# Written order on three more engines, and the accumulating weight transfer one tile later, in an SSD and gMLP step

## The chip, the cores and the metric

The kernel runs on one core of a Trainium2 chip. The metric is the device time of one execution in microseconds. The kernel before takes 1185.45 us (median of 3 runs, 1184.87 to 1282.32).

## What is computed

One inference step through two layers over 640 tokens: 512 of a prompt, and 8 running streams of 16 tokens. The width is 1024. The first layer is a Mamba-2 SSD mixer, the second a gMLP with spatial gating.

```
proj = h @ w_in                                   # z | x | B | C | dt
xbc_c = silu(causal_dwconv(xbc, conv_prev, w, b)) # width 4
la = cumsum(dt * a); decay = exp(causal(la_t - la_s))
y_in = einsum('btsg,btsgr,bsgr,bsgrp->btgrp', C B^T, decay, dt, x)
y_st = C h * exp(la);  h_new = h * exp(last) + B (w dt x)
y = gated_group_rms_norm(y + d_skip * x, z); out = y @ w_out
# second layer: u, v, z = h @ w_in; v = layer_norm(gelu(v))
# out = (gelu(u) * (w_spatial v + b) * silu(z)) @ w_out
```

Each of the two layers adds its result to the trunk. The 32 heads lie in 8 groups that share B and C; the states before and after the step are inputs and outputs. All data is f32.

## The kernel before, in words

**Products.** An f32 product is made of three matmuls: both operands are split into a high and a low part (xH, xL; wh, wl), and high by high, low by high and high by low are added in PSUM. A projection of one weight tile (128 x 1024) over the 640 tokens is 48 such matmuls (pin), in two halves of the tokens.

**Weights.** The class Stream hands out weight tiles in a fixed sequence. `wsplit` (L94 to L100) fetches one: GpSimd issues a transfer of 512 KB to wh (L97); ScalarE writes wl = -wh (L98), rounded as wh is; GpSimd issues the same transfer again, this time adding to wl (L99). `next()` hands out a tile and issues what is missing up to three tiles ahead. There are four buffers each for wh and wl, so a tile's wh can only be issued when PE has read the tile four places before it. In the sequence of a full group stand x0, x1, B, C, z0, o, o, z1: the two o are tiles of the output projection of the group before. At the end of the sequence stand 16 tiles wBv of the gMLP's v projection; three of them are fetched this way, and never read as such, since gMLP makes its own splits: a transfer to raw, a copy to wh on ScalarE (L815), the rest to wl on VectorE (L816).

**A group of heads** runs over these steps. `conv_tile` (from L402) takes the projection of x0, x1, B or C: GpSimd clears and copies the edges of a buffer xp (L405, L406), VectorE scales PSUM into xp (L407 to L409), GpSimd copies the last tokens out as new cache (L411, L412), ScalarE and VectorE convolve to acc (L414, L417), and ScalarE's tanh and VectorE make xc (L423, L424). PE transposes xc to token order (tp, L464). `decay` makes four tiles E, each by a transfer, five instructions and an exponential on ScalarE (L510, L511). After the projection of z0 come five steps (the list `ssd`): `prompt_states(0)`, whose first instruction after PE's st is a copy to hs on ScalarE (L557); `old_states`, where VectorE fills cz (L571), PE makes yq, and GpSimd multiplies the old states h by their decay, eight times (L582); `cb_prompt`; `prompt_states(1)`; `cb_sample`. The output pieces (pop, ten of them, each followed by a sum into the trunk on VectorE, L681) lie between them. `mask` multiplies E by CBm, on VectorE, and one of the four on GpSimd (L626); `pair(0)` and `pair(1)` make yB and yA from them. Between the two pairs lie the last five output pieces. `gate` (th, y, yHL, L670 to L675) closes a pair; the projection z1 comes after `pair(1)`.

**What sets the order.** PE's order is the written one everywhere. In the SSD part a scheduler orders VectorE, ScalarE, GpSimd and SyncE; the gMLP part is in written order throughout. An engine takes its instructions, the transfers it issues among them, in its own order. In gMLP, `forms.next(n)` hands out a split weight and issues the splits up to n ahead (ScalarE L743, VectorE L744); `out_weights` (L962) calls it four times before the ten output pieces.

Of the kernel before, what the change touches and what calls it, by code (L numbers as in the profile page):

```python
# [15 lines left out]
P = 128  # L16
# [24 lines left out]
def hybrid_step(ctx: ExitStack, tc: tile.TileContext, xin, xT0, cst, wdt, cache, wA, wAo, h0in, wB, wBv, wBo,  # L41
# [49 lines left out]

    def wsplit(src):  # L94
        H = wpool.tile([P, 1024], F32R, name="wh", tag="wh", bufs=4)
        L = wpool.tile([P, 1024], F32R, name="wl", tag="wl", bufs=4)
        G.dma_start(out=H, in_=src)  # L97
        S.activation(L, H.bitcast(F32), AF.Identity, scale=-1.0)  # L98
        G.dma_start(out=L, in_=src, accum_op=ALU.add)  # L99
        return H, L  # L100

    class Stream:
        def __init__(self, srcs, ahead):
            self.srcs, self.ahead, self.got, self.n = srcs, ahead, [], 0

        def fill(self, ahead):
            while len(self.got) < min(len(self.srcs), self.n + ahead):
                i = len(self.got)
                self.got.append(wsplit(*self.srcs[i]))


        def first(self, n, between):
# [12 lines left out]

        def next(self, ahead=None):
            self.fill(1 + (self.ahead if ahead is None else ahead))
            r = self.got[self.n]
            self.got[self.n] = None
            self.n += 1  # L130
            return r
# [8 lines left out]
    def norm_first(zp, rb):  # L140
        xH, xL = norm_tiles()
        xt = zp.tile([P, KD, NT], F32, name="xt")
        nc.sync.dma_start(out=csb[0][:, :8], in_=cst[:, :8])
        nc.sync.dma_start(out=xt[:, 0, :], in_=xT0[0])
        dw = zp.tile([P, KD, HEADS], F32, name="dw")
        nc.sync.dma_start(out=dw, in_=wdt)
        dHL = zp.tile([P, KD, 2, HEADS], F32R, name="dHL")
        S.copy(out=dHL[:, :, 0], in_=dw)
        V.tensor_tensor(out=dHL[:, :, 1], in0=dw, in1=dHL[:, :, 0].bitcast(F32), op=ALU.subtract)
        W = stream.first(2, lambda i: [nc.sync.dma_start(out=xt[:, k, :], in_=xT0[k]) for k in ((1,), range(2, KD))[i]])  # L150
        nc.sync.dma_start(out=csb[0][:, 8:], in_=cst[:, 8:NCST1])
        acc = [zp.tile([P, NT], F32, name=f"sqa{i}") for i in range(2)]
        for k in range(KD):
            w = C("nw0")[:, k:k + 1]
            S.activation(xH[:, k, :], xt[:, k, :], AF.Identity, scale=w)
            V.scalar_tensor_tensor(xL[:, k, :], xt[:, k, :], w, xH[:, k, :].bitcast(F32), ALU.mult, ALU.subtract)
        stream.fill(1)
        warm = ps_op.tile([P, 512], F32, name="warm", tag="op")
        for _ in range(13):
            mm(warm[:, :P], ones, ones)  # L160
        pdt, px0 = [[pool.tile([P, 512], F32, name="pin", tag=tag)[:, :b - a] for a, b in HALVES]
                    for pool, tag in ((ps_y, "y"), (ps_in, "in"))]

        def dt_step(k):
            lw = dHL[:, k].rearrange("p a h -> p (a h)")
            for (a, b), o in zip(HALVES, pdt):
                mm(o[:64], lw, xH[:, k, a:b], start=(k == 0), stop=False)
                mm(o[:64], lw, xL[:, k, a:b], start=False, stop=(k == KD - 1))

        dt_step(0)  # L170
        for k in range(KD):
            if k + 1 < KD:
                dt_step(k + 1)
            for h in range(2):
                in_proj_step(W, (xH, xL), px0[h], h, k)
        dtT = zp.tile([64, NT], F32, name="dtT")
        for (a, b), o in zip(HALVES, pdt):
            S.copy(out=dtT[:, a:b], in_=o[:64])
        for k in range(KD):
            if k < 2:  # L180
                S.activation(acc[k], xt[:, k, :], AF.Square, scale=1.0 / 32)
            else:
                S.activation(xt[:, k, :], xt[:, k, :], AF.Square, scale=1.0 / 32)
                (V if k % 2 else G).tensor_tensor(out=acc[k % 2], in0=acc[k % 2], in1=xt[:, k, :], op=ALU.add)
        V.tensor_tensor(out=acc[0], in0=acc[0], in1=acc[1], op=ALU.add)
        rs = small.tile([P, TT], F32, name="rs0")

        def fin():
            pms = ps_m.tile([P, TT], F32, name="pms", tag="m")
            for t in range(TT):  # L190
                mm(pms[:, t:t + 1], acc[0][:, t * P:(t + 1) * P], ones[:, 0:1])
            V.tensor_copy(rs, rsqrt(pms, EPS, TT))
            ptd = ps_m.tile([P, TT, HEADS], F32, name="ptd", tag="m")
            for t in range(TT):
                mm(ptd[:, t, :], dtT[:, t * P:(t + 1) * P], C("sel")[:64])
            return ptd

        def half(a, b):
            pb = ps_m.tile([P, 512], F32, name="pb", tag="m")
            for t in range(a // P, b // P):  # L200
                dg = zp.tile([P, P], F32, name="dg", tag="dg", bufs=2)
                V.tensor_scalar(dg, ident, rs[:, t:t + 1], None, ALU.mult)
                mm(pb[:, t * P - a:(t + 1) * P - a], ones, dg)
            S.copy(out=rb[:, a:b], in_=pb[:, :b - a])

        return (xH, xL), px0, rs, fin, half
# [102 lines left out]
        names += [p[0] for p in part]  # L309
        units += [p[1:] for p in part]  # L310
    units += wo(GROUPS - 2) + wo(GROUPS - 1)
    units += [(wBv[i],) for i in range(16)]
    stream = Stream(units, 3)


    with ExitStack() as ca:
# [9 lines left out]
        ptds = []  # L326
        side.append(lambda: ptds.append(norm_fin()))
        side += [lambda h=h: norm_half(*h) for h in HALVES]
        px1 = in_proj(stream.next(), xT, ps_op, "op", at=(2, 10, 12))
        ptd = ptds[0]  # L330
        nc.sync.dma_start(out=csb[1], in_=cst[:, NCST1:])

# [69 lines left out]
        def conv_tile(o0, o1, ft, j, cch, nconv):  # L402
            xp = w1.tile([P, 667], F32, name="xp", tag="xp")
            xps = xp[:, 515:667].rearrange("p (b j) -> p b j", j=19)
            G.memset(xp[:, 0:3], 0.0)  # L405
            G.tensor_copy(out=xps[:, :, 0:3], in_=cch[:, j])  # L406
            V.tensor_tensor(out=xp[:, 3:387], in0=o0, in1=rb[:, 0:384], op=ALU.mult)  # L407
            V.tensor_tensor(out=xp[:, 387:515], in0=o1[:, 0:128], in1=rb[:, 384:512], op=ALU.mult)
            V.tensor_tensor(out=xps[:, :, 3:19], in0=o1[:, 128:256].rearrange("p (b j) -> p b j", j=16),  # L409
                            in1=rb[:, 512:640].rearrange("p (b j) -> p b j", j=16), op=ALU.mult)  # L410
            G.tensor_copy(out=nconv[:, j, 0, :], in_=xp[:, 512:515])  # L411
            G.tensor_copy(out=nconv[:, j, 1:9, :], in_=xps[:, :, 16:19])  # L412
            acc = w1.tile([P, 667], F32, name="acc", tag="acc")
            S.activation(acc[:, 0:664], xp[:, 0:664], AF.Identity, scale=cw[:, 4 * ft:4 * ft + 1],  # L414
                         bias=cw[:, 128 + ft:129 + ft])
            for k in range(1, 4):
                V.scalar_tensor_tensor(acc[:, 0:664], xp[:, k:k + 664], cw[:, 4 * ft + k:4 * ft + k + 1], acc[:, 0:664],  # L417
                                       ALU.mult, ALU.add)
            xc = w1.tile([P, NT], F32, name="xc", tag="xc", bufs=5)
            accs = acc[:, 515:667].rearrange("p (b j) -> p b j", j=19)[:, :, 0:16]  # L420
            xcs = xc[:, 512:].rearrange("p (b j) -> p b j", j=16)
            for o, a in ((xc[:, :512], acc[:, :512]), (xcs, accs)):
                S.activation(o, a, AF.Tanh)  # L423
                V.scalar_tensor_tensor(o, o, 1.0, a, ALU.add, ALU.mult)  # L424
            return xc

        cio = conv_io(0)
        pB = in_proj(stream.next(), xT, ps_y, "y")
        xcs = [conv_tile(*o, ft, j, *cio) for j, (o, ft) in enumerate(((px0, 0), (px1, 1), (pB, 16)))]
        side += [cum_sums] + [lambda h=h: by_heads(*h) for h in HALVES]  # L430
        pC = in_proj(stream.next(), xT, at=(2, 9, 11))
# [5 lines left out]

        xcs.append(conv_tile(*pC, 24, 3, *cio))
        pend = {}
        for g in range(GROUPS):  # L440
            last = g == GROUPS - 1
            hsl = slice(4 * g, 4 * g + 4)
# [340 lines left out]
    with ExitStack() as cb_:  # L783
# [162 lines left out]
        def then(n=1):  # L946
            for _ in range(min(n, len(later))):
                later.popleft()()
# [11 lines left out]
            V.scalar_tensor_tensor(h1[:, t, dsl], ps, 0.5, h1[:, t, dsl], ALU.mult, ALU.add)  # L960

        def out_weights():  # L962
            w = [forms.next(3) for _ in range(4)]
            return w[:2], w[2:]

        def out_piece(Ws, ys, p, after=None):
# [14 lines left out]
        for g in range(GROUPS):  # L981
# [9 lines left out]
            for i in range(2):  # L991
                f = 2 * g + i
                if i and 0 < g < GROUPS - 1:
                    Ws = out_weights()
                    for p in range(2 * TT):
                        out_piece(Ws, groups[g - 1], p)
                        then()
                uu = wk.tile([P, NT], F32, name="uu", tag="uu", bufs=2)
                zz = wk.tile([P, NT], F32, name="zz", tag="zz", bufs=1)
                pa, pb = (ps_m.tile([P, 512], F32, name="pqa", tag="m")[:, :HT],  # L1000
# [206 lines left out]
```

## Time and profile before

| | |
|---|---|
| profiled execution, its own time | 1181.53 us |
| span of its trace | 1179.4 us |
| busy PE / VectorE / ScalarE / GpSimd | 1053.0 / 826.2 / 447.1 / 228.2 us |
| granted clock of PE, mean | 0.96 of full speed |
| SSD part | 0 to 678 us |
| gMLP part | from 692 us on |

Busy time is the sum of an engine's instructions; a busy engine need not be at its peak. How the table is read: PE does most of the work, and the rows further on show where it waits, and for what. A row of a timeline gives the start, the duration, the engine, the line, the output and inputs, the count and, in brackets, the idle time before it with what ended it.

### The profile page before, as it was taken

The page shows a single profiled execution, that of the slowest core. Times are in us where ns is not written, and L with a number is a line of the kernel's source. Part 1 is how long each engine was busy: PE and PEld are TensorE (multiplying, and loading weights), DVE is VectorE, ACT ScalarE, POOL GpSimd, SP SyncE. Part 2 cuts the span into 40 slices and gives each one's busy share as a digit, 9 for nine tenths or more (in the row PEclk, how much of TensorE's full clock was granted, in tenths as well). Part 3 has the DMA queues.
Part 4 walks back from the last instruction along what each step waited for, and adds up shares of the span by engine and source line. Part 5 has one row for each costly group of instructions (what it writes and reads, how often), then busy time and mean ns, then how long its engine had stood idle before and what let it go on. Part 6 is the DMA issues. An engine that isn't in the chain of part 4 may idle for free.

```text
span 1179.4 us, 16944 instructions
## 1 busy us (share of the span) xinstructions
PE 1053.0 (89%) x6387; PEld 945.2 (80%) x6387; DVE 826.2 (70%) x1533; ACT 447.1 (38%) x804; POOL 228.2 (19%) x412
## 2 busy tenths in 40 slices
PE   7998998798889889987978949998899999999996
PEld 6987797697688678786977738887889889888985
DVE  4767866656747646756666766656788888788886
ACT  6354425244144153152252234334534333324343
POOL 3243413313314214224134100000000000000000
PEclk8898999999999989999998969998999999999998
DMA  9497676675575585676756642221124224223222
GB/s 321 108 247 196 142 200 155 137 231 135 121 232 126 132 230 136 144 200 145 207 143 155 213 115 72 72 81 50 52 81 129 67 70 125 82 82 97 84 63 89
DMA packets 66865, 161.08 MB, mean 137 GB/s; under 512 B 10176, under 2 KB 28864, under 8 KB 66784
## 3 DMA queue, kind: packets, MB, share of 16 engines
q0 software_dynamic: 19008, 69.21, 25.6%
q1 hardware_dynamic: 47776, 90.78, 24.6%
q8 instruction: 51, 0.84, 0.3%
q14 instruction: 30, 0.25, 0.1%
HBM read 143.11 MB, written 16.86 MB: 136 GB/s over the span
## 4 chain that ended last, share of the span: by engine, by line
PE 29%; DVE 22%; DMA 19%; issue 16%; ACT 8%; POOL 5%; SPq 0%; POOLq 0%; ACTq 0%; DVEq 0%
PE pv L69 9%; DMA wh<-wAo 7%; PE pop L69 6%; PE pin L69 5%; DMA wh<-wA 4%; DVE wf L744 4%; DMA dhl<-hl 3%; PE pqb L69 2%; DMA E<-laD 2%; ACT wl L98 2%; PE pqc L69 2%; DMA out_sspS<-h 2%; POOL wl L99 2%; DVE h L960 2%; PE pqa L69 1%
## 5 line engine op out<-in xcount | busy, mean ns | idle before, releaser
L69 PE MATMUL pin<-xH,wh 128*128 128x384 f32 (+1 forms) x768 | 252.5, 329 | 0.1
L69 PE MATMUL pin<-xL,wh 128*128 128x384 f32 (+1 forms) x768 | 241.8, 315 | 0.0
L69 PE MATMUL pin<-xH,wl 128*128 128x384 f32 (+1 forms) x768 | 241.7, 315 | 0.0
L69 PEld LDWEIGHTS pin<-xH,wh 128*128 128x128 f32 x768 | 149.8, 195 | 7.9 <-issue 4.3
L69 PEld LDWEIGHTS pin<-xL,wh 128*128 128x128 f32 x768 | 149.9, 195 | 0.2
L69 PEld LDWEIGHTS pin<-xH,wl 128*128 128x128 f32 x768 | 149.1, 194 | 0.0
L98 ACT ACTIVATE wl<-wh 128x1024 fp32r<-128x1024 f32 x66 | 69.9, 1059 | 192.0 <-DMA wh<-wA 102.2
L69 PE MATMUL pop<-wh,yHL 128*128 128x512 f32 x320 | 105.8, 412 | 22.8 <-DVE hs L561 13.1
L69 PE MATMUL pop<-wf,yHL 128*128 128x512 f32 x480 | 116.3, 398 | 8.7 <-DVE h L960 8.1
L417 DVE SCALAR_TENSOR_TENSOR acc<-xp,cw,acc 128x664 f32<-128x664 f32 x96 | 91.9, 957 | 35.1 <-ACT acc L414 33.5
L69 PEld LDWEIGHTS pop<-wf,yHL 128*128 128x128 f32 x480 | 88.8, 188 | 34.2 <-DVE h L960 12.8
L743 ACT CAST wf<-raw 128x512 fp32r<-128x512 f32 x128 | 76.7, 617 | 78.7 <-PE pop L69 28.8
L744 DVE TENSOR_TENSOR wf<-raw,wf 128x512 fp32r<-128x512 f32 x128 | 87.9, 692 | 25.0 <-ACT wf L743 22.6
L69 PEld LDWEIGHTS pop<-wh,yHL 128*128 128x128 f32 x320 | 58.6, 192 | 40.3 <-DVE hs L561 15.7
L424 DVE SCALAR_TENSOR_TENSOR xc<-xc,acc 128x512 f32<-128x512 f32 x64 | 35.5, 594 | 59.4 <-ACT xc L423 59.3
L99 POOL DMA_DIRECT2D wl<-wA x47 | 41.3, 878 | 176.6 <-ACT wl L98 151.5
L681 DVE SCALAR_TENSOR_TENSOR h<-pop,rr,h 128x512 f32<-128x512 f32 x80 | 59.3, 745 | 12.2 <-PE pop L69 12.1
L69 PE MATMUL pqa<-xH,wf 128*128 128x320 f32 x256 | 64.3, 320 | 3.2 <-ACT v L836 3.2
L69 PE MATMUL pqb<-tf,wf 128*128 128x320 f32 x384 | 64.1, 316 | 2.5 <-DVE zz L1022 2.5
L69 PE MATMUL pv<-wh,xL 128*128 128x512 f32 x160 | 63.4, 396 | 1.0 <-DVE xL L227 1.0
L69 PE MATMUL pop<-wl,yHL 128*128 128x512 f32 x160 | 64.0, 400 | 0.0
L69 PE MATMUL pv<-wh,xH 128*128 128x512 f32 x160 | 63.8, 398 | 0.0
(225 smaller groups left out, 2051.6 us busy)
## 6 DMA issues: line engine op xcount, KB each, us to landing
wh<-wA POOLq DMA_DIRECT2D x47, 512.0 KB, 6.6
wl<-wA POOLq DMA_DIRECT2D x47, 512.0 KB, 6.5
raw<-wB SPq DMA_DIRECT2D x32, 512.0 KB, 3.9
E<-laD SPq DMA_DIRECT2D x32, 320.0 KB, 6.5
h<-h0in SPq DMA_DIRECT2D x16, 512.0 KB, 5.2
out_sspS<-h SPq DMA_DIRECT2D x16, 512.0 KB, 6.6
wh<-wAo POOLq DMA_DIRECT2D x16, 512.0 KB, 5.8
wl<-wAo POOLq DMA_DIRECT2D x16, 512.0 KB, 5.6
```

The source lines that it names most:

```text
L69: T.matmul(out, lhsT=lhsT, rhs=rhs, start=start, stop=stop, **kw)
L98: S.activation(L, H.bitcast(F32), AF.Identity, scale=-1.0)
L99: G.dma_start(out=L, in_=src, accum_op=ALU.add)
L417: V.scalar_tensor_tensor(acc[:, 0:664], xp[:, k:k + 664], cw[:, 4 * ft + k:4 * ft + k + 1], acc[:, 0:664], ALU.mult, ALU.add)
L424: V.scalar_tensor_tensor(o, o, 1.0, a, ALU.add, ALU.mult)
L681: V.scalar_tensor_tensor(h1[:, t, dsl], ps, rg[:, t:t + 1], h1[:, t, dsl], ALU.mult, ALU.add)
L743: S.copy(out=t[:, 0], in_=src)
L744: V.tensor_tensor(out=t[:, 1], in0=src, in1=t[:, 0].bitcast(F32), op=ALU.subtract)
L960: V.scalar_tensor_tensor(h1[:, t, dsl], ps, 0.5, h1[:, t, dsl], ALU.mult, ALU.add)
```

## The change

GpSimd runs in written order through the whole program; VectorE and ScalarE do so from the loop over the groups on. SyncE stays with the scheduler. The transfer that adds to wl, and the copy ahead of it, are written in a new function `low`, called when the next tile's wh is about to be issued. Two early calls of `next` reach less far ahead. The 16 tiles wBv are gone from the sequence. In conv_tile the memset moves to VectorE, the three small copies move to ScalarE, two of them behind the acc instruction. In gMLP `out_weights` issues no splits ahead; they are issued after the pieces from the second on.

```diff
-    def wsplit(src):
-        H = wpool.tile([P, 1024], F32R, name="wh", tag="wh", bufs=4)
-        L = wpool.tile([P, 1024], F32R, name="wl", tag="wl", bufs=4)
-        G.dma_start(out=H, in_=src)
-        S.activation(L, H.bitcast(F32), AF.Identity, scale=-1.0)
-        G.dma_start(out=L, in_=src, accum_op=ALU.add)
-        return H, L
...
+        def low(self):
+            if self.half:
+                H, L, src = self.half
+                S.activation(L, H.bitcast(F32), AF.Identity, scale=-1.0)
+                G.dma_start(out=L, in_=src, accum_op=ALU.add)
+                self.half = None
 
         def fill(self, ahead):
             while len(self.got) < min(len(self.srcs), self.n + ahead):
-                i = len(self.got)
-                self.got.append(wsplit(*self.srcs[i]))
+                self.low()
+                src, = self.srcs[len(self.got)]
+                H = wpool.tile([P, 1024], F32R, name="wh", tag="wh", bufs=4)
+                L = wpool.tile([P, 1024], F32R, name="wl", tag="wl", bufs=4)
+                G.dma_start(out=H, in_=src)
+                self.half = H, L, src
+                self.got.append((H, L))
...
-    units += [(wBv[i],) for i in range(16)]
...
-        px1 = in_proj(stream.next(), xT, ps_op, "op", at=(2, 10, 12))
+        px1 = in_proj(stream.next(1), xT, ps_op, "op", at=(2, 10, 12))
...
-            G.memset(xp[:, 0:3], 0.0)
-            G.tensor_copy(out=xps[:, :, 0:3], in_=cch[:, j])
+            V.memset(xp[:, 0:3], 0.0)
+            S.copy(out=xps[:, :, 0:3], in_=cch[:, j])
...
-            G.tensor_copy(out=nconv[:, j, 0, :], in_=xp[:, 512:515])
-            G.tensor_copy(out=nconv[:, j, 1:9, :], in_=xps[:, :, 16:19])
             acc = w1.tile([P, 667], F32, name="acc", tag="acc")
...
+            S.copy(out=nconv[:, j, 0, :], in_=xp[:, 512:515])
+            S.copy(out=nconv[:, j, 1:9, :], in_=xps[:, :, 16:19])
...
-        pB = in_proj(stream.next(), xT, ps_y, "y")
+        pB = in_proj(stream.next(2), xT, ps_y, "y")
...
+        ca.enter_context(tc.manual_schedule(engines={mybir.EngineType.DVE, mybir.EngineType.Activation}))
         for g in range(GROUPS):
...
-            w = [forms.next(3) for _ in range(4)]
+            w = [forms.next(0) for _ in range(4)]
...
                         out_piece(Ws, groups[g - 1], p)
                         then()
+                        if p:
+                            forms.fill(min(p // 2 + 1, 4))
...
-    with _tile.TileContext(nc) as tc, tc.manual_schedule(engines={_mybir.EngineType.PE}):
+    with _tile.TileContext(nc) as tc, tc.manual_schedule(engines={_mybir.EngineType.PE, _mybir.EngineType.Pool}):
```

The first place is GpSimd in a full group, from the wl of a tile ahead of z0's end to the wh after `pair(1)`. Before, word for word (the first wh is that of the next x0, the pair of wh behind E those of the next x1 and B):

```order
L99 DMA wl<-wA 128x1024
L97 DMA wh<-wA 128x1024
L582 TENSOR_TENSOR h_1903<-h_1903,etot 128x256 x2
L582 TENSOR_TENSOR h_1905<-h_1905,etot 128x256
L582 TENSOR_TENSOR h_1903<-h_1903,etot 128x256 x2
L582 TENSOR_TENSOR h_1905<-h_1905,etot 128x256 x3
L99 DMA wl<-wA 128x1024
L626 TENSOR_TENSOR E<-E,CBm 128x640
L97 DMA wh<-wA 128x1024 x2
```

The same place in the change (the wh are those of z1, the next x0, the next x1, and, behind E, the next B):

```order
L112 DMA wh<-wA 128x1024
L103 DMA wl<-wA 128x1024
L112 DMA wh<-wA 128x1024
L103 DMA wl<-wA 128x1024
L112 DMA wh<-wA 128x1024
L591 TENSOR_TENSOR h_1903<-h_1903,etot 128x256 x4
L591 TENSOR_TENSOR h_1905<-h_1905,etot 128x256 x4
L635 TENSOR_TENSOR E<-E,CBm 128x640
L103 DMA wl<-wA 128x1024
L112 DMA wh<-wA 128x1024
```

The eight products and E moved from ahead of the wh of the next x1 to behind it, and the wh of the next B from beside that wh to behind the next wl.

The second place is ScalarE in a full group, from z0 to the first gate (th). Before, word for word:

```order
L98 ACTIVATE wl<-wh 128x1024
L423 ACTIVATE xc<-acc 128x512
L423 ACTIVATE xc<-acc 128x128
L466 COPY Bt<-tp 128x128
L486 CAST hl<-Bt 128x128
L557 COPY hs<-st 128x256
L98 ACTIVATE wl<-wh 128x1024
L670 ACTIVATE th<-zr 128x640
```

The same place in the change (the two wl are those of z1 and the next x0, the wl behind y that of the next x1):

```order
L475 COPY Bt<-tp 128x512
L475 COPY Bt<-tp 128x128
L495 CAST hl<-Bt 128x128
L497 CAST hl<-xw 128x256
L102 ACTIVATE wl<-wh 128x1024 x2
L566 COPY hs<-st 128x256
L679 ACTIVATE th<-zr 128x640
L301 ACTIVATE yHL<-y,csb_97 128x640
L684 ACTIVATE y<-y 128x640
L102 ACTIVATE wl<-wh 128x1024
```

The copy hs moved behind the wl of the next x0.

## Rows read from the trace of the kernel before

**Rows 1.** The tile yA in three stretches: count, duration in ns, first and last start.

```profile
L69 PE MATMUL yA<-E,xdt x16: 272/273/273, 158.8 to 159.6; 128*64 128x128 f32 x16
L69 PE MATMUL yA<-E,xdt x16: 272/272/273, 322.8 to 323.6; 128*64 128x128 f32 x16
L69 PE MATMUL yA<-E,xdt x16: 272/273/273, 571.2 to 572.0; 128*64 128x128 f32 x16
```

**Rows 2.** PE's waits from 323.9 to 377.7: total us, times, longest.

```profile
PE tp L464 <- DVE xc L424: 6.0, 2, 4.1
```

**Rows 3.** Timeline of PE, 376 to 409.

```profile
377.66 1.03 PE L69 MATMUL st<-xw,Bt 128*128 128x256 f32 x4
...
380.31 1.07 PE L69 MATMUL yq<-h,cz 128*32 128x256 f32 x16 [0.23 <-DVE cz L571]
...
389.32 0.73 PE L69 MATMUL pop<-wh,yHL 128*128 128x512 f32 x2 [2.98 <-DVE CBm L591]
...
393.31 0.73 PE L69 MATMUL pop<-wh,yHL 128*128 128x512 f32 x2 [2.34 <-DVE hs L561]
...
406.56 0.44 PE L69 MATMUL yB<-E,xdt 128*64 128x128 f32 x4
406.83 1.04 PE L69 MATMUL yA<-E,xdt 128*64 128x128 f32 x16
```

**Rows 4.** Timeline of ScalarE, 340 to 400.

```profile
350.88 1.06 ACT L98 ACTIVATE wl<-wh 128x1024 fp32r<-128x1024 f32 x1 [3.00 <-issue]
351.85 0.81 ACT L423 ACTIVATE xc<-acc 128x512 f32<-128x512 f32 x2
352.56 1.56 ACT L510 ACTIVATE E<-E,la 128x128 f32<-128x128 f32 x5
354.03 0.72 ACT L511 ACTIVATE E<-E 128x640 f32<-128x640 f32 x1
...
379.61 0.37 ACT L557 COPY hs<-st 128x256 f32<-128x256 f32 x1
388.30 1.06 ACT L98 ACTIVATE wl<-wh 128x1024 fp32r<-128x1024 f32 x1 [8.32 <-DMA wh<-wA]
```

**Rows 5.** Timeline of GpSimd, 325 to 412.

```profile
352.90 0.87 POOL L97 DMA_DIRECT2D wh<-wAo  x1
...
379.49 0.89 POOL L97 DMA_DIRECT2D wh<-wA  x1
381.02 4.90 POOL L582 TENSOR_TENSOR h<-h,etot 128x256 f32<-128x256 f32 x8 [0.64 <-PE yq L69]
...
390.55 1.69 POOL L626 TENSOR_TENSOR E<-E,CBm 128x640 f32<-128x640 f32 x1
405.20 1.26 POOL L97 DMA_DIRECT2D wh<-wA  x2 [12.97 <-PE pop L69]
```

**Rows 6.** PE's waits over the whole span: total us, times, longest.

```profile
PE pt L224 <- issue: 14.4, 1, 14.4
...
PE pop L69 <- DVE h L960: 8.1, 6, 1.3
...
PE pqc L69 <- DVE c L1016: 4.9, 5, 2.0
```

**Rows 7.** The page's transfers: count, KB each, median us from issue to landing.

```profile
wh<-wA POOLq DMA_DIRECT2D x47, 512.0 KB, 6.6
...
raw<-wB SPq DMA_DIRECT2D x32, 512.0 KB, 3.9
```

**Rows 8.** Timeline of GpSimd, 60 to 165.

```profile
133.86 0.87 POOL L99 DMA_DIRECT2D wl<-wA  x1 [5.24 <-ACT Bt L466]
134.41 0.43 POOL L405 MEMSET xp<- 128x3 f32 x1
```

**Rows 9.** Timeline of VectorE, 126 to 136, and 678 to 693.

```profile
129.37 2.80 DVE L417 SCALAR_TENSOR_TENSOR acc<-xp,cw,acc 128x664 f32<-128x664 f32 x3 [1.01 <-ACT acc L414]
...
682.82 1.22 DVE L816 TENSOR_TENSOR wl<-raw,wh 128x1024 fp32r<-128x1024 f32 x1 [7.88 <-DMA wl<-wBv]
```

More of the change, by code (lines that the diff above doesn't have):

```diff
@@ L90, in rsqrt @@
         return r
-    def wsplit(src):
-        H = wpool.tile([P, 1024], F32R, name="wh", tag="wh", bufs=4)
-        L = wpool.tile([P, 1024], F32R, name="wl", tag="wl", bufs=4)
-        G.dma_start(out=H, in_=src)
-        S.activation(L, H.bitcast(F32), AF.Identity, scale=-1.0)
-        G.dma_start(out=L, in_=src, accum_op=ALU.add)
-        return H, L
     class Stream:
         def __init__(self, srcs, ahead):
-            self.srcs, self.ahead, self.got, self.n = srcs, ahead, [], 0
+            self.srcs, self.ahead, self.got, self.n, self.half = srcs, ahead, [], 0, None
+        def low(self):
[4 more added lines that the diff above has]
+                self.half = None
         def fill(self, ahead):
             while len(self.got) < min(len(self.srcs), self.n + ahead):
-                i = len(self.got)
-                self.got.append(wsplit(*self.srcs[i]))
+                self.low()
[5 more added lines that the diff above has]
+                self.got.append((H, L))
         def first(self, n, between):
@@ L127, in next @@
             self.fill(1 + (self.ahead if ahead is None else ahead))
+            if len(self.got) == len(self.srcs):
+                self.low()
             r = self.got[self.n]
@@ L157, in norm_first @@
         stream.fill(1)
+        stream.low()
         warm = ps_op.tile([P, 512], F32, name="warm", tag="op")
```

## The prediction

> **What bounds the kernel now.** I read PE's waits first, then the timelines of PE, ScalarE and GpSimd over one group of heads, then the transfers. The SSD part is eight groups; a group ends with the second block of yA multiplications. Those of the second, fourth and seventh group end at 159.9, 323.9 and 572.3 us [rows 1] (the last start in each row plus 0.27). Five full groups lie between 159.9 and 572.3, so one takes 82.5 us. In the group from 323.9 PE's only wait before z0's last multiplication is for the activated convolution, xc: 6.0 us [rows 2]. ScalarE shows why: at 350.88 its copy wl had stood until its wh transfer was there, and the tanh of xc ran behind it, at 351.85 [rows 4]. After z0 come yq at 380.31 and waits of 2.98 and 2.34 for VectorE [rows 3]. One gap of 14.4 stands between SSD and gMLP, and gMLP has six short waits for h, 8.1 [rows 6]. In these stretches PE works without a break otherwise, so what PE waits for sets the time.
>
> **What the change removes.** The accumulating half of a tile now comes one tile later, just ahead of the next tile's wh. Its wh has then landed while PE ran a projection, so the xc waits should go: 6.0 in the group shown. The copies of conv_tile move to ScalarE: three per tile, each below the 0.37 of the larger hs copy [rows 4], so at most 1.1 a tile. Two of them stand behind the acc instruction, while VectorE needs 2.80 for its three acc steps [rows 9]; the third needs nothing of PE and is done early. I cost them at nothing; without this cover they would cost at most 32 times 1.1, 35 us. VectorE's memset goes the same way.
>
> **What written order adds.** Three places, all seen in the order of the change.
>
> *ScalarE before yq.* Two wl copies now stand ahead of the hs copy; before, hs was first. The second waits for the wh of the next x0, which GpSimd can only issue once z0 has been consumed by PE and after the preceding wl. VectorE's hs steps and h sum stand ahead of cz, which yq needs. From that issue to yq: landing 6.6 [rows 7], wl 1.06, hs copy 0.37, then four small VectorE steps, which I estimate from hs at 0.37 each: 9.5 us. Today hs ran at 379.61, and the wl that would stand ahead of it at 388.30 [rows 4].
>
> *GpSimd before the second pair.* The wh of x1 waits for the last out-projection piece that reads its buffer; it was issued at 405.20. Ahead of it, at 381.02 and 390.55, ran the eight h products (4.90) and the mask E (1.69) that the second pair needs [rows 5]. Now they stand behind it: 405.20 + 0.63 (half of the two issues) + 4.90 + 1.69 = 412.4, where PE's yB wanted E at 406.56 [rows 3]: a wait of 5.9. So from yq to the group's end I take 27.56 (380.31 to 406.83 + 1.04) less 2.98 and 2.34, which lie under the later yq, plus 5.9: 28.1.
>
> *The chain of transfers.* GpSimd alternates: wl of one tile (waits for ScalarE's copy, which waits for wh's landing), then wh of the next. One cycle is landing 6.6 [rows 7] plus copy and two issues: 350.88 (copy starts) to 352.90 (next wh issued) is 2.0 [rows 4, 5]. So c = 8.6. The four wh issues from 352.90 to 379.49 [rows 5] are 8.9 apart, so c is about this long already now. After the pair the next wl stands behind the first gate on ScalarE and VectorE: nine steps, about 0.7 each by the exponential of 128x640 [rows 4], 6.4, then copy and issues 2.0: the wh of B leaves 8.4 us after the group's end, where now two are issued together before it. From B six cycles (B, C, z0, two o, z1) lead to the wh of x0.
>
> So a group takes 8.4 + 6 x 8.6 + 9.5 + 28.1 = 97.6, against 82.5: **+15.1**, five times 75.5. Without the chain, z0 would end at 377.66 - 323.9 - 6.0 = 47.8; the chain reaches that point only at 60.0, so it decides.
>
> By the Trainium skill (DMA: Bandwidth & Descriptors, section Anatomy of one DMA — SWDGE (gpsimd) path) a transfer that GpSimd issues takes about 2.0 us plus its bytes at 436 GB/s, for 512 KB an estimate of 3.2; the trace has 6.6 for this very transfer. With 3.2 the chain would not decide (rival A).
>
> **Bounds of c.** Below: the 512 KB transfer raw<-wB lands in 3.9 [rows 7], c = 5.9. Above: the wh issued at 379.49 had its copy at 388.30, 8.8, c = 10.8. I take 8.6, since the median is over 47 transfers of the same kind.
>
> **The other parts.** *Second group* (the one that ends at 159.9): the two blocks alone give (9.5 - 2.65, the present way from z0's end to yq) + 5.9 = 12.8. Its four E decays now stand ahead of a wl: 4 x (1.56 + 0.72) = 9.1 [rows 4], plus a cycle: 30.5 at most. I take 22. *First group*: the decays stand there too; between 0 and 17.7 (9.1 + c); I take 10. *Last group*: it has no transfers to fetch behind hs and loses its xc waits; I take nothing, between -5.9 and +5.9 (one mask block). *Gap of 14.4*: VectorE stood 7.88 in it for the wl of a gMLP tile that is no longer fetched there [rows 9]; I take -8, between 0 and -14.4. *gMLP splits*: they stood between VectorE's h sums; spreading them over the pieces can remove the 8.1, or move it to the product pqc, which waits 4.9 now [rows 6]; I take -4, between -8.1 and +4.9.
>
> Sum: 75.5 + 22 + 10 + 0 - 8 - 4 = +95.5. The profiled execution took 1181.5 us, 0.3% below the median of the runs shown (1185.45). 1181.5 + 95.5 = **1277 us**.
>
> **Rivals.** *A, transfers land quickly.* If less traffic around them brings wh down to 3.9, the chain needs 8.4 + 6 x 5.9 = 43.8 and z0 decides at 47.8; yq comes at 47.8 + 9.5 - 2.7 = 54.6, the group ends at 82.7: +0.2. With the second group at 22 - 2 x 2.7 = 16.6 and the first at 7.3 the sum is 1 + 16.6 + 7.3 - 12 = +13: 1194. It holds below a landing of 4.6 ((47.8 - 8.4) / 6 - 2.0). For it: raw<-wB. Against it: wl and wh are issued back to back, and 47 of them show 6.6. By the skill's 3.2 a group would take 82.0, and the whole about 1191.
>
> *B, landings as long as the last one.* c = 10.8 makes a group 110.8: +141.5 for five, 1343. For it: 8.8 at 379.49. Against it: the median.
>
> *C, GpSimd's products pass a waiting transfer.* If a DMA that waits did not hold what stands behind it, the mask block would be gone and each wh would leave as its buffer comes free: group 47.8 + 9.5 + 22.2 = 79.5, -3.0; second group +6.9, first 0, the rest -12: 1181.5 - 15 + 6.9 - 12 = 1161. This decides from one point: whether an elementwise instruction starts while a DMA ahead of it waits. Against it: the memset of xp ran at 134.41, right behind the transfer issued at 133.86 after 5.24 us of waiting, though the VectorE acc steps that could hold its buffer had ended by 129.37 + 2.80 = 132.2 [rows 8, 9]. By the Trainium skill (TensorE: Matmul & The Clock Gate, section on the array's architectural detail) GpSimd's queue is strictly first in, first out; the memset agrees.
>
> **How the numbers follow.** Forecast (1240 to 1325, c from 7.4 to 8.9 with the other bounds): 0.62. Between A and it (1210 to 1240): 0.10. A: 0.13. B and worse: 0.08. C: 0.07. The range from 1190 to 1325 leaves out B and C, 0.15. Two per cent is about what a measurement of this kernel can tell from no change. Slower: 0.62 + 0.10 + 0.08 = 0.80; same: A, 0.13; faster: C, 0.07.
>
> **What would show it.** Right: tp's waits for xc nearly gone; PE's yq waiting 6 us or more for cz in every full group, with ScalarE's wl ahead of hs waiting for wh; yB waiting some 6 us for GpSimd's E, behind a wh that waited for pop; wh issues 8.6 apart after each pair; groups of about 98; the gap before pt at 6. Wrong: groups below 85, landings below 4.6, or E on GpSimd starting before the wh ahead of it was issued. The sum is most exposed to the landing: one us of it moves five groups by 35 us.

## The result

The changed kernel takes 1392.71 us (median of 4 runs, 1390.23 to 1395.19), before 1185.16 us; the ratio is 1.1769, with a 95% interval from 1.1722 to 1.1816. The median of the kernel before counts one execution of 1282.32 us in a slower state; the ratio leaves it out. The direction was forecast (slower), the size was not: 1277 was predicted, with 1325 as the upper end. The profiled execution's span is 1390.1 us against 1179.4, 210.7 more.

PE's waits over the whole span of the changed kernel (total us, times, longest):

```profile
PE yq L69 <- DVE cz L580: 103.5, 8, 16.8
PE yB L69 <- POOL E L635: 29.5, 6, 4.9
PE st L69 <- ACT Bt L475: 29.5, 6, 7.0
PE pin L69 <- DVE zr L548: 26.0, 2, 18.7
PE pin L69 <- DVE xp L414: 24.4, 8, 3.6
PE pin L69 <- DMA wl<-wA: 18.6, 11, 3.7
...
PE pt L232 <- issue: 1.6, 1, 1.6
```

No wait of tp for xc is left, and the gap ahead of pt [rows 6] is 1.6. Both were promised. In their place stand yq's waits for cz and yB's for GpSimd's E, at the very places that were forecast, and three kinds that were not: st for Bt, pin for zr and pin for xp.

The ends of the second, fourth, fifth, seventh and eighth group, read as with [rows 1] from the tile yA of the changed kernel (count, duration in ns, first and last start):

```profile
L69 PE MATMUL yA<-E,xdt x12: 420/421/421, 220.2 to 221.4; 128*64 128x128 f32 x12
L69 PE MATMUL yA<-E,xdt x12: 421/421/422, 446.7 to 448.0; 128*64 128x128 f32 x12
L69 PE MATMUL yA<-E,xdt x15: 420/421/421, 558.0 to 559.7; 128*64 128x128 f32 x15
L69 PE MATMUL yA<-E,xdt x12: 421/421/421, 781.4 to 782.7; 128*64 128x128 f32 x12
L69 PE MATMUL yA<-E,xdt x16: 272/272/273, 876.8 to 877.6; 128*64 128x128 f32 x16
```

Last start plus duration gives 221.8, 448.4, 560.1, 783.1 and 877.9; the first group ends at 125.8. The five full groups take 112.3 us each ((783.1 - 221.8) / 5) against 82.5. So the 210.7 us lie here:

| stretch | before | after | difference | predicted |
|---|---|---|---|---|
| up to the end of the first group | 106.3 | 125.8 | +19.4 | +10 |
| second group | 53.5 | 96.1 | +42.6 | +22 |
| five full groups | 412.4 | 561.2 | +148.8 | +75.5 |
| last group | 82.7 | 94.8 | +12.1 | 0 |
| from there to pt | 37.7 | 34.3 | -3.4 | -8 |
| from pt to the end | 486.8 | 477.9 | -8.9 | -4 |

One group, from 448.4 to 560.1, follows the predicted walk. GpSimd's timeline in it (the answers to [rows 5]):

```profile
455.99 0.88 POOL L112 DMA_DIRECT2D wh<-wA  x1
...
465.75 0.87 POOL L112 DMA_DIRECT2D wh<-wA  x1
...
495.94 0.88 POOL L112 DMA_DIRECT2D wh<-wAo  x1
...
507.21 0.89 POOL L103 DMA_DIRECT2D wl<-wAo  x1 [8.36 <-ACT wl L102]
...
516.76 0.90 POOL L103 DMA_DIRECT2D wl<-wA  x1 [8.09 <-ACT wl L102]
517.31 0.90 POOL L112 DMA_DIRECT2D wh<-wA  x1
...
551.03 0.55 POOL L112 DMA_DIRECT2D wh<-wA  x1 [22.00 <-PE pop L69]
551.59 4.60 POOL L591 TENSOR_TENSOR h<-h,etot 128x256 f32<-128x256 f32 x8
556.16 1.52 POOL L635 TENSOR_TENSOR E<-E,CBm 128x640 f32<-128x640 f32 x1
```

The wh of B leaves at 455.99, 7.6 us after the group's end (8.4 predicted). From there to the wh of the next x0 at 517.31 are six cycles, 61.3 us: 10.2 a cycle (8.6 predicted); the other four full groups, taken the same way, have 10.4 to 10.7. The last three rows are the block ahead of the second pair, as foreseen: 22.00 of waiting for pop, then the products and E. ScalarE and PE close the group, first ScalarE's timeline, then PE's:

```profile
505.75 1.04 ACT L102 ACTIVATE wl<-wh 128x1024 fp32r<-128x1024 f32 x1
...
515.28 1.06 ACT L102 ACTIVATE wl<-wh 128x1024 fp32r<-128x1024 f32 x1 [7.22 <-DMA wh<-wA]
526.67 1.06 ACT L102 ACTIVATE wl<-wh 128x1024 fp32r<-128x1024 f32 x1 [10.34 <-DMA wh<-wA]
527.63 0.35 ACT L566 COPY hs<-st 128x256 f32<-128x256 f32 x1
```

```profile
529.79 1.93 PE L69 MATMUL yq<-h,cz 128*32 128x256 f32 x16 [16.50 <-DVE cz L580]
...
557.73 0.47 PE L69 MATMUL yB<-E,xdt 128*64 128x128 f32 x1 [4.91 <-POOL E L635]
```

The hs copy stands behind a wl that waited 10.34 us for its wh, which landed some 9.3 us after its issue at 517.31. yq comes 12.5 us after that issue (9.5 predicted), the group's end 30.3 after yq (28.1 predicted). 7.6 + 61.3 + 12.5 + 30.3 = 111.7.

### The profile page after: what moved, and what is told of

The parts are those of the page before. It is cut to its first block, busy times and chain, and to the rows that moved or that the text cites. A ratio compares the mean times of both kernels' runs of the same rounds, so it can differ in the third digit from the quotient of the medians.

```text
span 1390.1 us, 16915 instructions
## 1 busy us (share of the span) xinstructions
PE 1093.6 (79%) x6387; PEld 973.8 (70%) x6387; DVE 828.7 (60%) x1565; ACT 456.4 (33%) x897; POOL 198.3 (14%) x278
## 3 DMA queue, kind: packets, MB, share of 16 engines
q0 software_dynamic: 18144, 66.07, 21.4%
## 4 chain that ended last, share of the span: by engine, by line
issue 35%; PE 30%; DVE 15%; POOL 10%; DMA 5%; ACT 4%; SPq 0%; POOLq 0%; DVEq 0%; ACTq 0%
PE pop L69 9%; PE pv L69 7%; DMA wh<-wA 4%; PE pin L69 3%; PE pqb L69 3%; POOL xw L485 3%; POOL h L591 2%; DVE wf L753 2%; POOL wl L103 2%; PE pqc L69 2%; POOL wh L112 2%; PE pqa L69 2%; DMA wh<-wAo 1%; DVE h L969 1%; ACT wf L752 1%
## 5 line engine op out<-in xcount | busy, mean ns | idle before, releaser
L69 PE MATMUL pin<-xH,wh 128*128 128x384 f32 (+1 forms) x768 | 258.4, 336 | 50.5 <-DVE zr L548 26.0
L69 PE MATMUL pin<-xH,wl 128*128 128x384 f32 (+1 forms) x768 | 246.9, 321 | 18.6 <-DMA wl<-wA 18.6
L69 PE MATMUL pin<-xL,wh 128*128 128x384 f32 (+1 forms) x768 | 245.6, 320 | 0.0
L69 PEld LDWEIGHTS pin<-xH,wh 128*128 128x128 f32 x768 | 152.7, 199 | 61.3 <-DVE zr L548 26.4
L424 DVE SCALAR_TENSOR_TENSOR acc<-xp,cw,acc 128x664 f32<-128x664 f32 x96 | 108.9, 1134 | 67.4 <-ACT acc L419 65.4
L102 ACT ACTIVATE wl<-wh 128x1024 fp32r<-128x1024 f32 x63 | 66.3, 1052 | 190.3 <-DMA wh<-wA 135.2
L69 PE MATMUL pop<-wh,yHL 128*128 128x512 f32 x320 | 111.9, 433 | 6.6 <-DVE h L690 6.6
L69 PE MATMUL yq<-h,cz 128*32 128x256 f32 x128 | 14.6, 603 | 103.5 <-DVE cz L580 103.5
L569 DVE TENSOR_TENSOR hs<-hs,etot 128x256 f32<-128x256 f32 x24 | 10.3, 430 | 119.5 <-ACT hs L566 119.2
L69 PEld LDWEIGHTS yq<-h,cz 128*32 128x32 f32 x128 | 4.6, 152 | 109.6 <-DVE cz L580 106.2
L69 PEld LDWEIGHTS pop<-wh,yHL 128*128 128x128 f32 x320 | 64.4, 208 | 21.9 <-DVE h L690 7.2
```

The lines of the kernel that those rows point to most:

```text
L69: T.matmul(out, lhsT=lhsT, rhs=rhs, start=start, stop=stop, **kw)
L569: V.tensor_tensor(out=hs[:, t], in0=hs[:, t - 1], in1=ev, op=ALU.mult)
```

## The experiments

My theory after the result: nothing but the written order costs time, and it does so where long work, or a transfer that waits, stands ahead of short work that PE waits for. The rivals: the transfer that adds, one tile later, is itself at fault; one engine's order alone is; or the chain alone is. The table has, for each run, the first group's end, the second group, a full group (mean of five) and the last, all from the yA tiles, and the time. Where a ratio is given below, it is to executions of the kernel before that ran alongside (medians 1180.2 to 1182.82); e2 to e6 and e11 are one execution each, and only differences far above the spread of the changed kernel's four (1390.23 to 1395.19) are read from them.

| run | first | second | full | last | time, us |
|---|---|---|---|---|---|
| before | 106.3 | 53.5 | 82.5 | 82.7 | 1185.16 |
| after | 125.8 | 96.1 | 112.3 | 94.8 | 1392.71 |
| e1, all but the written order | 105.8 | 59.6 | 82.3 | 79.1 | 1162.34 |
| e2, GpSimd written | 110.8 | 61.3 | 90.7 | 80.1 | 1218.78 |
| e3, VectorE and ScalarE written | 122.3 | 72.3 | 82.0 | 81.3 | 1195.02 |
| e4, wh ahead of wl | 119.1 | 83.5 | 97.1 | 85.8 | 1280.5 |
| e5, late fetches | 124.6 | 73.0 | 90.1 | 95.6 | 1258.2 |
| e6, e4 and e5 | 123.1 | 72.7 | 85.0 | 84.7 | 1213.35 |
| e7, e3 from the third group, decays late | 107.8 | 58.0 | 83.2 | 82.9 | 1168.68 |
| e9, e7 with late fetches and one earlier wl | 105.0 | 56.0 | 75.0 | 83.4 | 1127.95 |
| e10, e9 with GpSimd written, wh ahead of wl | 107.4 | 55.6 | 75.0 | 85.0 | 1129.57 |
| e11, after with decays late | 129.8 | 95.5 | 109.4 | 96.0 | 1381.94 |

**All edits but the written order.**

```diff
-        ca.enter_context(tc.manual_schedule(engines={mybir.EngineType.DVE, mybir.EngineType.Activation}))
...
-    with _tile.TileContext(nc) as tc, tc.manual_schedule(engines={_mybir.EngineType.PE, _mybir.EngineType.Pool}):
+    with _tile.TileContext(nc) as tc, tc.manual_schedule(engines={_mybir.EngineType.PE}):
```

> All edits of the change except the written order: GpSimd, VectorE and ScalarE stay with the scheduler. Theory 1 (the written order alone costs the time, by where it puts three things; the other edits are small gains): 1140 to 1175 us, faster than before by the gap between the parts (8 to 12), the gMLP waits (about 9) and some of the 27 us of xc waits. Rival (the transfer that adds, one tile later, is itself what makes weights late): above 1250 us.

1162.34 us, as expected, ratio 0.9845 (0.9789 to 0.9901): the written order costs 230 us, the other edits together gain about 18. The transfer that adds, one tile later, is not at fault. But it brings nothing in the full groups either, 82.3 against 82.5:

```profile
PE tp L470 <- DVE xc L430: 32.4, 10, 6.5
```

The waits for xc are about what they were (6.0 in the one group of [rows 2], 27.9 in the five full groups here, 5.6 each). The scheduler still puts a wl copy that waits for its transfer ahead of the tanh, as ScalarE's timeline shows:

```profile
276.14 1.06 ACT L101 ACTIVATE wl<-wh 128x1024 fp32r<-128x1024 f32 x1 [3.72 <-issue]
...
277.73 0.81 ACT L429 ACTIVATE xc<-acc 128x512 f32<-128x512 f32 x2
```

So the later transfer takes these waits away only together with ScalarE's written order: they stay in the next run, which leaves ScalarE to the scheduler, and are gone in the one after it, which does not.

**GpSimd alone in written order** (the change without the VectorE and ScalarE line of the diff above).

> The change with VectorE and ScalarE left to the scheduler; GpSimd in written order. Theory 1: the wait of yB for E on GpSimd (4.9 us, six times) stays, the chain of wl and wh on GpSimd stays, the wait of yq for cz (16 us in a full group) shrinks below 5, since the hs copy may pass the wl copies: 1290 to 1330 us. Rival (ScalarE's and VectorE's written order is all of it): below 1200 us.

1218.78, below the 1290 to 1330 expected. The block ahead of the second pair is there, in the amount of the changed kernel, 4.9 of the 8.2 us that a full group loses:

```profile
PE yB L69 <- POOL E L634: 29.5, 6, 4.9
PE tp L472 <- DVE xc L431: 27.2, 15, 6.9
...
PE yq L69 <- DVE cz L579: 3.4, 4, 1.8
```

yq hardly waits: with ScalarE scheduled, hs does not stand behind the wl copies, and GpSimd's chain of transfers does not set the group.

**VectorE and ScalarE alone in written order** (the change without the GpSimd part).

> The change with GpSimd left to the scheduler; VectorE and ScalarE in written order. Theory 1: yB's wait for GpSimd's E goes, yq's wait for cz stays at 8 to 16 us, since hs stands behind the two wl copies: 1270 to 1340 us. Rival (GpSimd's written order is all of it): below 1200 us.

1195.02, below the 1270 to 1340 expected, and below the 1200 that the rival named. But the rival's reason, that GpSimd's order is all of it, does not hold either: alone it costs 8 us a group. yq's waits are 6.2 in all, not 8 to 16 in a group. GpSimd's timeline shows why: the scheduler puts wh ahead of the wl of earlier tiles, each wh leaving as PE frees its buffer.

```profile
317.54 0.55 POOL L112 DMA_DIRECT2D wh<-wA  x1 [4.79 <-PE pin L69]
...
319.45 0.92 POOL L103 DMA_DIRECT2D wl<-wAo  x1
325.60 0.57 POOL L112 DMA_DIRECT2D wh<-wA  x1 [5.22 <-PE pin L69]
...
331.38 1.82 POOL L103 DMA_DIRECT2D wl<-wA  x2 [1.34 <-ACT wl L102]
```

So each order alone costs 8 us (GpSimd) or nothing (VectorE, ScalarE) in a full group, and both together 30. What the two make together, and neither alone, is, as I read it, the closed chain, which the next runs test: wl on GpSimd waits for ScalarE's copy, the next wh waits behind that wl, the next copy waits for that wh, and hs waits behind the copy. The loss of the first and second group, 19 and 43, is in good part VectorE's and ScalarE's: 16 and 19 here.

**The chain cut.**

```diff
             while len(self.got) < min(len(self.srcs), self.n + ahead):
-                self.low()
                 src, = self.srcs[len(self.got)]
...
                 G.dma_start(out=H, in_=src)
+                self.low()
                 self.half = H, L, src
```

> The change with one exchange in fill: the wh transfer of the next tile is issued ahead of the copy and the adding transfer of the tile before. So a wh no longer waits for ScalarE's copy. Theory 1: the chain of 10.2 us per tile is cut; a full group falls from 112 to about 91 us (z0's end at 48, yq 12.5 later, 30.3 from there), the whole to 1250 to 1290 us; waits of pin for wl<-wA vanish. Rival (the chain is not what sets the group, only the two blocks do): within 15 us of 1392.

1280.5, inside the range. But a full group falls from 112.3 to 97.1 and not to 91, and pin's waits for wl<-wA do not vanish (3.3 left of 18.6). yq's waits fall from 103.5 to 31.2. With the two blocks still there, the chain is worth 15 us a group, and this one exchange brings back 112 of the 207 us lost. The two transfers also change places in how long they take. After, then the exchange:

```profile
wh<-wA POOLq DMA_DIRECT2D x47, 512.0 KB, 7.4
wl<-wA POOLq DMA_DIRECT2D x47, 512.0 KB, 5.6
```

```profile
wh<-wA POOLq DMA_DIRECT2D x47, 512.0 KB, 5.4
wl<-wA POOLq DMA_DIRECT2D x47, 512.0 KB, 6.7
```

Each of these medians mixes transfers that leave alone with transfers that leave right behind another, so I sorted them by that. In the changed kernel 55 of the 63 wh leave within 0.9 us behind a wl, and all 55 land after it; the 39 of them from wA have a median of 7.7. In e4 nine wl from wA leave that close behind a wh, and all nine land after it, with a median of 7.2 for the wh's 4.2. What else is under way counts too. Three wh of the changed kernel, each with the stretch that was asked for: one alone (551 to 556), one behind a wl (495.9 to 502.5), and the one of 465.75, behind a wl while other transfers moved 1.41 MB (465.7 to 475.6):

```profile
wh<-wA POOLq DMA_DIRECT2D x1, 512.0 KB, 3.8
```

```profile
wh<-wAo POOLq DMA_DIRECT2D x1, 512.0 KB, 6.5
```

```profile
q1 hardware_dynamic: 552, 1.41, 46.6%
...
wh<-wA POOLq DMA_DIRECT2D x1, 512.0 KB, 9.7
```

(The q1 row has packets, MB and share of the queue for transfers that GpSimd does not issue.) In the full groups the five wh that leave alone land in 3.7 to 3.9. Of the 35 behind a wl, the 15 with at most 0.12 MB of other queues' traffic during their flight take 6.0 to 7.1, the 20 with 0.39 MB or more 7.3 to 11.1.

**The two blocks removed.**

```diff
-                Wo = [stream.next(), stream.next()]
+                Wo = [stream.next(2), stream.next(1)]
...
                 ssd[1]()
+                stream.fill(2)
                 ssd[2]()
...
             mask(1)
+            if 0 < g < GROUPS - 1:
+                stream.fill(3)
```

> The change with two fetches written later in the five full groups and the second: the wh of the next x0 (and wl of z1) behind old_states, the wh of the next x1 behind mask(1). So the hs copy has no new wl ahead of it, and the h products and E have no wh ahead of them that waits for an output piece. The chain wl to wh stays. Theory 1 (chain plus two blocks): yB's wait for GpSimd's E gone, yq's wait below 6; the chain then holds the o tiles, whose wl is needed for the piece ahead of yq: group 88 to 95 against 112, the whole 1240 to 1290. Rival (the chain alone sets the group): group above 105, above 1350.

1258.2, a full group 90.1, both as expected; yB no longer waits for GpSimd, and yq's waits are 12.2 in all. What is left over the whole span is st's waits for Bt (26.9), pin's for zr (24.3), for xp (23.7) and for wl<-wA (21.4). The next run, which also cuts the chain, shows which of them belong to it.

**Chain and blocks removed.**

> The late fetches and the exchange of wh and wl together, all still in written order. Theory 1: the 97 us per group that the exchange leaves, less the 5.3 of yq and the 5.8 of yB seen there: 84 to 88 a group, the whole 1195 to 1225 us. Rival (the time lies in ScalarE's own load, the E decays ahead of Bt): group above 93, above 1245.

1213.35, a full group 85.0, as expected. All three engines are still in written order, and 27 of the 30 us of a full group are gone. Against the run before, pin's waits fall from 23.7 to 7.2 for xp and from 21.4 to 10.6 for wl<-wA, so these were for the most part the chain's; st's for Bt and pin's for zr stay. With the blocks gone, cutting the chain is worth 5 us a group (90.1 to 85.0) where it was worth 15 with them: chain and blocks overlap, and their shares do not add up. What remains over the scheduled kernel is in the first two groups (123.1 and 72.7, against 105.8 and 59.6), in the last (84.7 against 79.1) and in st's waits for Bt, which stands behind two E decays on ScalarE:

```profile
PE st L69 <- ACT Bt L475: 31.5, 6, 5.6
```

**Written order from the third group on, GpSimd scheduled.**

```diff
+            if g == 2:
+                ca.enter_context(tc.manual_schedule(engines={mybir.EngineType.DVE, mybir.EngineType.Activation}))
...
-                queue(2, *((0, 1, 2, 3) if g == 1 else (2, 3)))
+                queue(2, *((0, 1, 2, 3) if g == 1 else (2, 3) if last else ()))
...
                 ssd[1]()
+                if g > 1:
+                    decay(2)
+                    decay(3)
                 ssd[2]()
```

> GpSimd left to the scheduler; VectorE and ScalarE in written order from the third group on, not from the first; and the decays of E for the third and fourth head written behind old_states instead of ahead of the Bt copies. Theory 1 (written order costs only where long work stands ahead of short work that PE waits for): the first two groups as scheduled, st's wait for Bt (4 us a group) gone, full groups 77 to 81: 1130 to 1155 us. Rival (the wait moves to E or to the output weights): full groups 82 or more, 1160 or more.

1168.68, ratio 0.9905 (0.9874 to 0.9937). The first two groups are back (107.8 and 58.0), and st's waits for Bt are gone. But the full groups stay at 83.2 and the time is above the range: a miss. The rival's numbers came, though not quite its reason: the wait moved to the output weights only in part, and most of it to yq, six times:

```profile
PE yq L69 <- DVE cz L581: 28.9, 6, 5.9
PE pop L69 <- DMA wl<-wAo: 12.4, 6, 2.9
```

ScalarE had Bt out early, and then stood with hs behind the second wl again.

**That wait removed too.** The late fetches are added, and the wl copy of the second o tile moves ahead of C's convolution:

```diff
                 o = in_proj(stream.next(), xT, at=(3, 7, 11, 14))
+                if g > 1:
+                    stream.low()
                 xcs.append(conv_tile(*o, 24 + g, 3, *cio))
```

> As the run with VectorE and ScalarE written from the third group on and the two decays behind old_states, now with the fetches of the next x0 and x1 written late (behind old_states, behind mask) and the wl copy of the second o tile ahead of C's convolution. GpSimd stays scheduled. Theory 1: yq's wait for cz (5.5 in a full group, hs behind two wl copies) and pop's wait for wl of the o tile (2.4) go: full groups 74 to 77, the whole 1125 to 1145 us. Rival (PE's other work or the landing of wl takes their place): full groups 80 or more, 1155 or more.

1127.95, ratio 0.9565 (0.9524 to 0.9606): faster than both kernels. A full group takes 75.0, 7.5 us less than before the change. In the group from 236.4 to 310.7 PE waits 4.2 us in all:

```profile
PE pin L69 <- DMA wl<-wA: 1.4, 2, 1.2
PE yB L69 <- DVE E L642: 1.0, 2, 0.7
PE yq L69 <- DVE cz L583: 0.9, 1, 0.9
PE pop L69 <- DMA dhl<-hl: 0.9, 1, 0.9
```

**The same with GpSimd written as well,** from the third group on, and wh ahead of wl:

> The same with GpSimd in written order too, from the third group on, and the wh of a tile issued ahead of the wl before it. Theory 1: with nothing long ahead of what PE waits for, written order on GpSimd costs nothing either: within 10 us of the same kernel with GpSimd scheduled, 1125 to 1150. Rival (written order on GpSimd costs 9 us a group whatever stands where): 1170 or more.

1129.57, ratio 0.9564 (0.9521 to 0.9608), a full group 75.0. In the full groups of this kernel written order on three engines costs nothing, once what waits stands behind what is awaited. The run makes two edits at once, so it does not show what each would do alone.

**How much of the cycle is ScalarE's lateness.** The changed kernel, with only the two decays moved behind old_states (as in the diff of the run from the third group on):

> The change with one move: in the full groups the E decays of the third and fourth head stand on ScalarE behind old_states instead of ahead of the wl copy of the second o tile. Theory 1 (the chain takes 10.2 us per tile, because a wh that is issued behind a wl lands in 7.4, and because in two of six cycles ScalarE is late by 1.4 and 3.3): the 3.3 goes and st's wait for Bt, 4 us, goes under: full groups 107 to 109 against 112, the whole 1365 to 1380 us. Rival (ScalarE's lateness does not matter, since the landing ends later anyway): within 5 us of 1392.

1381.94 and 109.4 a group: 2.9 of the 3.3 us expected in a group, the time 2 us above the range. The waits of st for Bt fell from 29.5 to 11.8 in all, while yq's stayed at 102.2 (103.5 before the move) and pop's for the wl of the o tiles rose from 8.3 to 16.5. So the earlier st brought nothing of its own: PE waits at the next places of the chain instead.

**Two parts alone, on the kernel before.** Without the wBv tiles (the line `units += [(wBv[i],) for i in range(16)]` deleted):

> The kernel before without the 16 gMLP tiles at the end of the fetch sequence, nothing else. Theory 1: the gap before pt falls from 14.4 to some 3, with VectorE's wait of 7.9 for wl<-wBv gone, the rest as before: 8 to 13 us faster, 1167 to 1175. Rival (the gap has another cause, the h sums of the last output pieces): within 3 us of before.

1169.92, ratio 0.9906 (0.9873 to 0.994), as expected; the gap ahead of pt, 14.4 before [rows 6], is 1.6.

With only the gMLP splits moved between the pieces:

> The kernel before with the gMLP splits between the output pieces, nothing else. Theory 1: the six waits of pop for h, 1.35 each, go and no other wait grows: 6 to 10 us faster than before, 1173 to 1178. Rival (the waits move to the product pqc or pqb): within 3 us of before.

1170.67, ratio 0.9916 (0.9892 to 0.994). That is 10.0 less than the 1180.67 alongside, at the upper end of the 6 to 10 expected; the time itself lies below the range, which was reckoned from a slower median of the kernel before. Of the six waits for h (8.1) 0.2 is left, and pqc's are 4.3 against 4.9 [rows 6].

## Why the prediction was right or wrong

**Right: the mechanism and its places.** hs behind the wl of the next x0, E behind the wh that waits for pop, and the chain of wl and wh between them were read from the order, and the trace has all three; e4, e5 and e6 take them away and give back 27 of the 30 us of a full group. Rival C fell: the products started at 551.59, right behind the wh that had waited 22.00 us for pop, though yq had freed the old states at about 531.7. So did rival A: the landing went up, not down. The xc waits went, as the first part said. One term at nothing held only because other waits covered it: the copies and the memset of conv_tile. pin waits 24.4 for xp in the changed kernel; in the full groups that lies ahead of yq's wait and, by e6, belongs mostly to the chain.

**Wrong: the length of the cycle, and with it the range.** Of the 210.7 us, 95.5 were predicted. The other 115 are 73 in the five full groups, 30 in the first two, 12 in the last, and 5 in the gap, less 5 that the gMLP splits gave beyond their term. Of the 29.8 us that a full group lost, 15.1 were predicted. In the group shown the terms are: cycle 10.2 for 8.6 (six times 1.6, 9.7), issue to yq 12.5 for 9.5 (3.0), yq to the end 30.3 for 28.1 (2.2), the gate 7.6 for 8.4 (-0.8): 14.1 in all. The step that failed is "landing 6.6 ... So c = 8.6", with the copy taken as never late. By cause, the landings are 7.2 of the 14.1: 7.4 on average in the six cycles (4.5 in all) and 9.3 ahead of yq (2.7), both for 6.6. A late ScalarE is 4.7, PE's clock 2.2, and the rest cancels.

- *The median was of the wrong mixture.* 6.6 was the median of 47 wh transfers issued in any company before. The prediction says that wl and wh are issued back to back and that 47 of them show 6.6; but only 14 of the 47 left right behind a wl, and these had a median of 7.9, the other 33 one of 5.1. In the changed order every wh of the cycles leaves 0.6 us behind a wl. So the longer landing could have been read before the change, and the traffic of the other queues belongs to it (e4). No run takes that traffic away, so its share is not measured by itself.
- *Rival B came close by luck.* Its group of 110.8 is near the measured 112.3, but it rests on a cycle of 10.8, where 10.2 was measured; and its step to yq kept the landing of 6.6, though 8.8 was its own premise (with it: 113.0). B also had no late ScalarE and no slower clock. It was given 0.08, together with what is worse.
- *ScalarE is part of the cycle.* I took the copy to be waiting for the landing. In two of six cycles ScalarE itself is late, behind the exponentials: the wl copies at 493.87 and 505.75, which let the transfers of 495.34 and 507.21 go, start 1.4 and 3.3 us after their wh had landed. The second share was taken away by a run, which gave back 2.9 us a group (e11).
- *The clock of PE.* I costed nothing for it. From yq to the end of the group PE is busy 24.50 us for 22.27 in the same 141 instructions, and the granted clock is 0.84 of full speed for 0.94. From yq to the group's end, in the two groups shown, the rows are, before and after:

```profile
380.30:407.90 27.60, 22.27 (x141) 17.89 (x141) 18.63 (x31) 3.18 (x4) 8.57 (x13) 0.94 0.58 125
```

```profile
529.80:560.20 30.40, 24.50 (x141) 19.47 (x141) 14.71 (x27) 0.74 (x1) 6.64 (x10) 0.84 0.18 46
```

(Columns: the stretch, its us, busy us and instructions of PE, PE's weight loads, VectorE, ScalarE and GpSimd, granted clock, share and GB/s of the transfers.) The 2.2 us by which the step from yq missed are just this: PE's idle time in it is 5.90, where the estimate was 5.9, all of it for yB, whose wait is 4.91.

**Wrong: the first, second and last group.** I had bounded the first two by four decays and a cycle, and the last by one mask block. The first shows what was overlooked, VectorE's own order: the copy hl stood 15.22 us for ScalarE, which had the decays and a wl first, and zr stood behind it, while PE waited 18.66 for zr to empty its PSUM.

```profile
79.87 0.29 DVE L496 TENSOR_TENSOR hl<-Bt,hl 128x128 fp32r<-128x128 f32 x1 [15.22 <-ACT hl L495]
...
84.31 0.88 DVE L548 TENSOR_TENSOR zr<-pin,rb 128x384 f32<-128x384 f32 x2
```

I had followed the queues of ScalarE and GpSimd, and of VectorE only the steps ahead of cz. e7 and e3 set against each other show what the written order of VectorE and ScalarE does there together: with it from the third group on, the first two groups are back at 107.8 and 58.0, from 122.3 and 72.3. No run parts the two engines, and the second group's own waits were not taken apart by a run. The last group I took at nothing because no transfer is fetched behind hs; it lost 12.1. Its largest wait (783.1 to 877.9) is of the same kind as the first group's, and the prediction had no such term; waits of 3.4 for cz and 2.9 for wl<-wA stand beside it:

```profile
PE pin L69 <- DVE zr L548: 7.4, 1, 7.4
```

The group falls to 85.8 when the chain is cut (e4), where the waits for cz and wl all but go and the one for zr stays at 6.8. So the chain reaches into the last group as well, and VectorE's wait for zr remains, as it does in e3 (5.1).

**The small terms.** The gap was mis-sized the other way: it fell from 14.4 to 1.6, but a wait of 5.9 of the output pieces for VectorE's h came ahead of it, so the stretch gained 3.4 for the 8 taken (another wait of 1.7, for VectorE's y, and 1.8 of slower PE make up the rest). In e4 the wait for h is gone, and the stretch is 11.0 shorter than before the change. The gMLP splits gained 8.9 for 4: the waits did not move elsewhere. Alone on the kernel before, the two parts give 11 to 13 and 10 us.

## What to carry to other kernels

An order written by hand is fixed for the slowest thing in it: put an instruction that waits for a transfer, or for a buffer, behind the short work that another engine is waiting for, and issue a fetch ahead of, not behind, the transfer whose data still has to pass an engine. Here two orders that cost 8 and 0 us a group each cost 30 together, because only together did they close a loop through a transfer, and set the step that PE waits for behind it (e5 leaves the loop, moves that step away, and a group takes 90); so look for loops over engines and queues, not for waits on one. Price such a loop with durations read at places where the same two transfers are issued in the same order and the other queues are as busy, not with the median of the line; look whether an engine in the loop is itself late; and let the range reach to the longest landing seen.

## What was not expected of the hardware

Of two transfers of 512 KB that GpSimd issues within 0.9 us the second landed later every time in the changed kernel (55 of 55 wh behind a wl) and in e4 (nine of nine wl behind a wh), so which of the two is on the path matters. A wh alone landed in 3.7 to 3.9 us in the full groups, behind a wl in 6.0 to 11.1, the more the busier the other queues were. Over the whole kernel PE's granted clock fell from 0.96 to 0.902, and its busy time for the same 6387 matmuls rose from 1053.0 to 1093.6 us: a fifth of the 207 us lost is PE working more slowly, not waiting. In the group shown the clock was at its lower level, 1.2 GHz (0.50 granted), in the 5.1 us right behind yq's wait of 16.50 us, and at full speed (1.00) in the 20.5 us after that. The first of these stretches, with the columns as above:

```profile
529.80:534.90 5.10, 5.10 (x28) 3.54 (x29) 1.15 (x3) 0.00 (x0) 0.00 (x0) 0.50 0.58 104
```
